# Attention's output projection by seven products with fewer accumulating transfers, another price for their queue in the plan, and the columns of sinks written by ScalarE or VectorE

## The chip, the cores and the metric

The kernel runs on one core of a Trainium2 chip. The metric is the device time of one execution in microseconds. Three executions of the kernel before took 2039.61, 2040.94 and 2041.01 us; the median is 2040.94 us. Line numbers are those of the kernel before.

## What is computed

A network of two layers on 1024 tokens of width 1024, in float32: layer 0 mixes by sliding-window attention with sinks, layer 1 by a gated recurrence (HGRN2), and each is followed by an MLP with a squared ReLU. The change lies in layer 0's attention:

```python
qkv = h @ w_qkv + b_qkv                       # 16 query heads of 64, 4 key/value heads
scores = einsum(q_blocks, k_band) * HEAD_DIM ** -0.5      # a block of 128 tokens sees itself and the block before
m = maximum(max(scores, axis=-1), sink)
e = exp(scores - m)
probs = e / (sum(e, axis=-1) + exp(sink - m))
out = einsum(probs, v_band)
x = x + out.reshape(bsz, seq, Q_DIM) @ w_o    # the output projection
x = x + square(relu(rmsnorm(x) @ w_up)) @ w_down
```

## The kernel before, in words

**Products.** TensorE (PE) multiplies float32 as three passes of a rounded high part and a low rest (`mm3`, L505): high by high, high by low, low by high. Every operand is therefore split into two tiles: ScalarE (ACT) casts the high part, VectorE (DVE) subtracts it (`weight_split` for weights into tiles `wh` and `wl`, `split` for activations). A tile is 128 by 512, or 256 KB.

**Seven products.** The output projection (`o_proj`, L1473) takes 2 by 2 blocks of tokens and channels by a scheme of seven products in place of eight (Strassen's, in Winograd's form). Products 1, 2 and 4 use blocks of the weight as they are; 5, 6, 3 and 7 use sums of blocks: 5 the sum of two, 6 the same with a third added, 3 the same with the fourth added, 7 another sum of two. The order is 1, 2, 5, 3, 6, 7, 4 (L1476), each over four slices `p` of the contracted channels, with four banks of PSUM each: products 1, 2, 5, 6 and 7 in the banks `p` (the list `main`), products 3 and 4 in the banks `q` (the list `side`). `proj_weight` (L1454) makes a weight: the sums are made by transfers. `dma_sum` (L455) loads the first block through SyncE's queue (SP) and adds the others with accumulating transfers, `dma_add` (L452), which GpSimd (POOL) issues: the transfer reads the destination and writes the sum back. For each `p`, product 5 has one such transfer, 6 one more into the same tile, 3 three, and 7 one: 24 in all. The tile of product 5 (`kept[p]`) goes on to product 6.

The operands of the token side are sums too: tiles `t[p]` and `b11[p]` get other heads' outputs added, 14 times by `dma_add` and twice by VectorE. A part of the residual `x` is added by 8 more accumulating transfers.

**Attention around it.** `attend` (L1381) goes through four groups of four heads, two groups at a time (a pair `gp`), in two halves of the tokens. The queries of a pair are written to DRAM by the projection (`queries`, `rows_out`, L1276) in ten stores, and read back in eight loads of 256 KB (the stacks) when the pair begins. `attend_block` (L1413) handles one block of one group: a tile `m` out of six buffers holds the scores, and its last column the sinks, which POOL writes (`self.ts("Pool", ...)`, L1419); then come the scores on PE, copies and masks on ACT and DVE, the exponentials, the transposes, and in `values` the products with the values. For the second half of the tokens, `attention` (L1563) interleaves the blocks with the last slices of the QKV products and with the first products of the output projection. After them the MLP's operands are made (`mlp_first`, and `finish`, which also uses accumulating transfers, tiles `t`).

**The order.** All of this is written into a list, and a planner (`Schedule`, L160) turns it into one order: a forward pass over modelled engines with a cost for each operation, then a backward pass that gives each a latest time, four times over. `SUM` is the time from the end of a `dma_add`'s issue to its landing, `LOAD` and `STORE` those of SP's transfers; the third argument of `self.op` before the tiles' own is the time on the issuing queue (900 for a `dma_add`). Engines take their instructions in the order planned, and one that waits holds all behind it on its engine. Tiles come from a fixed number of buffers (`a` 60, `t` 18, `m` 6, `wr` 6, four banks each of `p` and `q`), so the plan also sets who waits for a buffer.

Of the kernel before, what the change touches and what calls it, by code (L numbers as in the profile page):

```python
# [15 lines left out]
ALU = mybir.AluOpType  # L16
AX = mybir.AxisListType

P = 128
# [4 lines left out]
TH = T // NH  # L24
# [113 lines left out]
WEIGH = 1.0  # L138
DRAIN = {"whole": 200.0, "columns": 200.0}
LOAD, STORE = 4200.0,3200.0  # L140
SUM = 6400.0
HALF = {"ACT": 125.0, "DVE": 105.0}
READERS = {"ACT": "DVE", "DVE": "ACT"}
TABLES = {AF.Sqrt: "sqrt", AF.Sin: "sin", AF.Exp: "exp", AF.Tanh: "exp"}
# [239 lines left out]
class Net:  # L384
    def __init__(self, ctx, tc, io):
        self.nc, self.io = tc.nc, io
        self.s = Schedule()
        self.n = 0
        self.x = None
        self.pool = ctx.enter_context(tc.tile_pool(name="sb", bufs=1))  # L390
        self.pp = ctx.enter_context(tc.tile_pool(name="ps", bufs=1, space=bass.MemoryType.PSUM))
        self.dram = ctx.enter_context(tc.tile_pool(name="dr", bufs=1, space=bass.MemoryType.DRAM))
        nc = self.nc
        self.par = self.const((P, N_PAR))
        self.ones = self.const((P, P))
        self.memset(self.ones, 1.0)
        self.mean = self.const((P, 1))
        self.memset(self.mean, 1.0 / D)
        self.eps = self.const((P, 1))
        self.memset(self.eps, EPS)  # L400
        zero = self.t(F32, (P, P))
        self.memset(zero, 0.0)
        self.warm(zero)
        self.ident = self.const((P, P))
        self.square = [self.const((P, BPH)) for _ in range(NH)]
        self.op("Pool", nc.gpsimd.affine_select, [self.ident], [zero], 300,
                self.ident, zero, [[-1, P]], ALU.not_equal, 1.0, base=0, channel_multiplier=1)
# [15 lines left out]
    def a(self, dt=F32, shape=(P, TH)):  # L423
        return self.tile("a", BUFS["a"], shape, dt)
# [22 lines left out]

    def dma(self, out, in_, nbytes, least=450.0, late=0.0):
        tail = LOAD if isinstance(out, View) and out.buf.tag[0] != "d" else STORE
        self.op("SP", self.nc.sync.dma_start, [out], [in_], max(least, nbytes / 320.0), out, in_, tail=tail + late)  # L450

    def dma_add(self, out, y):  # L452
        self.op("Pool", self.nc.gpsimd.dma_start, [out], [out, y], 900.0, out, y, accum_op=ALU.add, tail=SUM)

    def dma_sum(self, out, x, *more):  # L455
        self.dma(out, x, 4 * P * TH)
        for y in more:
            self.dma_add(out, y)

# [953 lines left out]
    def attend_block(self, g, n, stacks):  # L1413
# [2 lines left out]
        tok = slice((n % BPH) * P, (n % BPH) * P + P)  # L1416
        ks, kl = self.ks[i][g].only(*((m, k) for m in (n - 1, n) for k in (0, HD))), self.kl[i][g].only(n - 1, n, "o")
        m = self.t(F32, (P, 4, P + 2), "m")
        self.ts("Pool", m[:, :, P : P + 1], self.sink[:, 4 * g : 4 * g + 4].unsqueeze(2), 1.0, None, ALU.mult, None, 4)  # L1419
        scores = [self.psum("q").rearrange("p (h s) -> p h s", h=2) for _ in range(2)]  # L1420
        for h in range(4):
            self.mm(scores[h // 2][:, h % 2], stacks[h][:, tok], ks[:, c], h % 2 == 0, False, 2 * P)
# [20 lines left out]
        if n:  # L1443
            y = self.t(F32, (P, 4, P))
# [9 lines left out]
    def proj_weight(self, name, p, kept):  # L1454

        a = lambda i, k: self.io["wo"][k, p, :, i]
        self.s.lead = LEAD
        if name in (1, 2, 4):
            z = self.raw(a(*{1: (0, 0), 2: (0, 1), 4: (1, 1)}[name]))
        elif name == 5:  # L1460
            z = kept[p] = self.a()
            self.dma_sum(z, a(1, 0), a(1, 1))
        elif name == 6:
            z = kept[p]
            self.dma_add(z, a(0, 0))
        else:
            z = self.a()
            self.dma_sum(z, a(0, 0), a(1, 0), *((a(1, 1), a(0, 1)) if name == 3 else ()))
        w = self.weight_split(z)
        self.s.lead = 0  # L1470
        return w

    def o_proj(self, out, b):  # L1473
# [3 lines left out]
        main = [self.psum() for _ in range(HK)]  # L1477
# [59 lines left out]
        yield from product(3, side, True)  # L1537
        yield from product(6, main, False)
        for m in range(HK):
            z = self.a()  # L1540
            self.copy(z, main[m])
            self.dma_add(z, self.io["x"][1, m])
            later.append(z)
        for m in range(HK):
            self.x[m][1] = later[m]
# [17 lines left out]
    def attention(self, layer):  # L1563
        self.v, self.dv, self.ks, self.kl = [], [], [None] * 3, [None] * 3
        out = [{}, {}]
        ahead = self.first_loads()
        h = [self.scaled(layer, 0)]
        self.attention_constants()
        run(self.qkv(0, *h[0], ahead))
        self.load_x([1])  # L1570
        h.append(self.scaled(layer, 1))
        rest = self.qkv(1, *h[1])
        for k, _ in enumerate(self.attend(0, out[0])):
            for _ in range((k + 1) * 18 // 16 - k * 18 // 16):
                next(rest)
        tiles = [[out[0][2 * k + p // 2, p % 2] for p in range(HK)] for k in range(2)]
        proj, first = self.o_proj(out, tiles), self.mlp_first(layer)
        side = chain(rest, proj)
        left = 6 + 13
        for k, _ in enumerate(self.attend(1, out[1])):  # L1580
            for _ in range((k + 1) * left // 16 - k * left // 16):
                next(side)
        for k in range(14):
            next(proj)
            if k % 3 == 2:
                next(first)
        run(proj)
        run(first)


    def hgrn_constants(self):
# [513 lines left out]
def run(pieces):  # L2105
    for _ in pieces:
        pass
# [92 lines left out]
```

## Time and profile before

| what | value |
|---|---|
| median of three runs | 2040.94 us |
| the profiled execution's own time | 2040.05 us |
| its span, first to last instruction | 2038.3 us |
| PE busy in the span | 2001.9 us, 98% |
| DVE, ACT and POOL busy | 1803.7, 1316.2 and 125.7 us |
| accumulating transfers (queue q0) | 24.65 MB, 6.9% of the 16 DMA engines' span |
| all of SP's transfers (queue q1) | 503.99 MB, 73.0% |
| mean granted clock of PE | 0.993 |

In the trace, names of tiles stand without their numbers (`a`, `t`, `m`, `q`), `in_wo` is the weight of the output projection, `in_up` that of the MLP, `d` a tile in DRAM, `out<-in` the direction. `POOLq` and `SPq` are issues of transfers. Nearly all instructions have line 438, since one helper issues them, so they are told apart by engine, tiles and time. The attention with its output projection lies between about 85 and 312 us of the span, the first MLP's products begin at about 314 us.

### The profile page before, as it was taken

Reading aid. Unit: us, or ns where it says so; the run is one execution under the profiler, and the core shown is the slowest. Engines: PE = TensorE matmul, PEld = TensorE weight load, DVE = VectorE, ACT = ScalarE, POOL = GpSimd, SP = SyncE. Lnnn points to the kernel's source line nnn. Section 1 sums busy time; section 2 is a strip of 40 time slices with the busy share of each in tenths; the row PEclk is TensorE's granted clock in tenths of the full one; section 3 lists DMA queues with packets and bytes.
Section 4 is the critical chain, followed back from the end, with each engine's and each line's share of the span. In section 5 each row is a group of like instructions: output and inputs, shape, how many; then the busy total and the mean of one; then the engine's idle time right before and its main releaser. Section 6 shows DMA issues by size and latency. Waiting matters only on the chain.

```text
span 2038.3 us, 40062 instructions
## 1 busy us (share of the span) xinstructions
PE 2001.9 (98%) x13772; PEld 1698.9 (83%) x13772; DVE 1803.7 (88%) x3639; ACT 1316.2 (65%) x2765; POOL 125.7 (6%) x223
## 2 busy tenths in 40 slices
PE   9999898999999999999999999999899999999998
PEld 8887676899998888888888888888789999888887
DVE  7878778999998978989999999999899999887985
ACT  7777766767766544656666666766776777444573
POOL 2001431000001000000000000001000001100000
PEclk9999899999999999999999999999999999999999
DMA  7848999888879977855888888989888889996812
GB/s 247 268 143 242 250 203 281 270 278 282 294 259 342 335 244 236 276 168 175 282 282 286 284 293 310 316 299 313 271 273 288 270 290 289 349 314 213 268 58 84
DMA packets 296348, 531.23 MB, mean 261 GB/s; under 512 B 34256, under 2 KB 42832, under 8 KB 296144
## 3 DMA queue, kind: packets, MB, share of 16 engines
q1 hardware_dynamic: 282464, 503.99, 73.0%
q0 software_dynamic: 13536, 24.65, 6.9%
q8 instruction: 109, 1.79, 0.4%
q14 instruction: 95, 0.78, 0.1%
q10 hardware_dynamic: 144, 0.02, 0.0%
HBM read 412.04 MB, written 110.72 MB: 256 GB/s over the span
## 4 chain that ended last, share of the span: by engine, by line
PE 89%; DMA 4%; DVE 4%; ACT 2%; issue 1%; SPq 0%; POOL 0%; DVEq 0%; ACTq 0%; POOLq 0%
PE p L438 48%; PE q L438 41%; DMA d<-t 2%; DVE t L438 2%; ACT t L438 1%; DMA a<-d 1%; DVE m L438 1%; DVE wl L438 1%; DMA a<-in_wo 1%; DMA a<-a 0%; ACT a L438 0%; DVE a L438 0%; ACT wh L438 0%; SPq L438 0%; DMA a<-in_x 0%
## 5 line engine op out<-in xcount | busy, mean ns | idle before, releaser
L438 PE MATMUL p<-a,wh 128*128 128x512 f32 (+1 forms) x3056 | 852.1, 363 | 4.8 <-ACT a L438 4.5
L438 PE MATMUL q<-a,wh 128*128 128x512 f32 x2084 | 650.1, 393 | 12.5 <-ACT t L438 10.4
L438 PEld LDWEIGHTS p<-a,wh 128*128 128x128 f32 x3056 | 544.3, 189 | 90.8 <-ACT a L438 5.2
L438 PE MATMUL p<-a,wl 128*128 128x512 f32 (+1 forms) x1528 | 549.1, 362 | 0.4 <-DVE wl L438 0.4
L438 PEld LDWEIGHTS q<-a,wh 128*128 128x128 f32 x2084 | 388.4, 189 | 92.5 <-ACT t L438 12.1
L438 PE MATMUL q<-a,wl 128*128 128x512 f32 x1040 | 405.1, 391 | 0.0
L438 PEld LDWEIGHTS p<-a,wl 128*128 128x128 f32 x1528 | 287.7, 189 | 43.6 <-DVE wl L438 0.8
L438 ACT CAST wh<-m 128x512 fp32r<-128x512 f32 (+1 forms) x354 | 212.5, 604 | 159.7 <-PE q L438 93.0
L438 ACT CAST wh<-wr 128x512 fp32r<-128x512 f32 (+1 forms) x304 | 180.8, 602 | 140.0 <-PE p L438 86.4
L438 DVE TENSOR_TENSOR wl<-m,wh 128x512 fp32r<-128x512 f32 (+1 forms) x354 | 235.2, 668 | 39.7 <-ACT wh L438 35.9
L438 PEld LDWEIGHTS q<-a,wl 128*128 128x128 f32 x1040 | 196.3, 189 | 41.0
L438 DVE TENSOR_TENSOR wl<-wr,wh 128x512 fp32r<-128x512 f32 (+1 forms) x304 | 200.3, 664 | 34.1 <-ACT wh L438 29.1
L438 DVE TENSOR_TENSOR t<-t,t 128x512 f32<-128x512 f32 (+3 forms) x382 | 215.8, 586 | 12.5 <-DMA t<-d 5.8
L438 ACT ACTIVATE t<-t 128x512 f32<-128x512 f32 x294 | 184.0, 631 | 48.8 <-DVE t L438 44.1
L438 DVE TENSOR_TENSOR a<-t,a 128x512 fp32r<-128x512 f32 (+1 forms) x261 | 173.6, 684 | 17.9 <-PE q L438 8.5
L438 ACT CAST a<-t 128x512 fp32r<-128x512 f32 x181 | 109.3, 617 | 43.5 <-DMA t<-d 26.4
L438 DVE TENSOR_TENSOR t<-t,p 128x256 f32<-128x256 f32 x288 | 116.9, 415 | 17.2 <-PE p L438 13.8
L438 ACT COPY t<-q 128x512 f32<-128x512 f32 (+2 forms) x254 | 111.7, 442 | 25.6 <-PE q L438 16.4
L438 ACT CAST a<-a 128x512 fp32r<-128x512 f32 x140 | 85.4, 620 | 42.2 <-DVE a L438 39.5
L438 DVE TENSOR_TENSOR a<-a,a 128x512 fp32r<-128x512 f32 (+2 forms) x157 | 105.0, 679 | 6.9 <-ACT a L438 3.8
L438 DVE TENSOR_TENSOR m<-wr,wr 128x512 f32<-128x512 f32 (+1 forms) x152 | 97.2, 642 | 1.8 <-DMA wr<-in_up 1.3
L438 PE MATMUL p<-t,wh 128*128 128x256 f32 x480 | 90.7, 283 | 0.0
(142 smaller groups left out, 2364.9 us busy)
## 6 DMA issues: line engine op xcount, KB each, us to landing
t<-d SPq DMA_DIRECT2D x584, 256.0 KB
a<-d SPq DMA_DIRECT2D x350, 256.0 KB
d<-t SPq DMA_DIRECT2D x318, 256.0 KB
wr<-in_up SPq DMA_DIRECT2D x172, 256.0 KB
wr<-in_down SPq DMA_DIRECT2D x160, 256.0 KB
wr<-in_win SPq DMA_DIRECT2D x68, 256.0 KB
d<-a SPq DMA_DIRECT2D x64, 256.0 KB
wr<-in_wqkv SPq DMA_DIRECT2D x48, 256.0 KB
```

The source lines that it names most:

```text
L438: fn(*[place(a) for a in args], **{k: place(v) for k, v in kw.items()})
```

## The change

- `proj_weight`: product 3's weight is no longer summed by transfers. Its fourth block is loaded raw, and VectorE adds it to `kept[p]` (the sum of three that product 6 uses) into a tile `m`. Product 6's accumulating transfer is listed right after product 5's weight has been split, not when product 6's weight is asked for. The 24 accumulating transfers become 12, SP's loads stay 24.
- `o_proj`: four of the eight residual tiles are loaded through SP and added by VectorE from PSUM, where before ScalarE copied the product and an accumulating transfer added `x`.
- `attend_block`: the 32 columns of sinks are copies by ScalarE or VectorE, as the planner chooses, not by POOL (as planned: 22 and 10).
- the plan: a `dma_add` costs 2050 on POOL (900 before) and lands 4000 after that (6400 before); the first load of a `dma_sum` is given 1500 more; every SP transfer listed between the first QKV pass and the end of `attention` 1500 more (`slow`). These numbers change no work, only the order, in the whole program.

```diff
-SUM = 6400.0
+SUM, SLOW = 4000.0, 1500.0
...
-        self.op("SP", self.nc.sync.dma_start, [out], [in_], max(least, nbytes / 320.0), out, in_, tail=tail + late)
+        self.op("SP", self.nc.sync.dma_start, [out], [in_], max(least, nbytes / 320.0), out, in_, tail=tail + late + self.slow)
...
-        self.op("Pool", self.nc.gpsimd.dma_start, [out], [out, y], 900.0, out, y, accum_op=ALU.add, tail=SUM)
+        self.op("Pool", self.nc.gpsimd.dma_start, [out], [out, y], 2050.0, out, y, accum_op=ALU.add, tail=SUM)
...
-        self.dma(out, x, 4 * P * TH)
+        self.dma(out, x, 4 * P * TH, late=1500.0)
...
-        self.ts("Pool", m[:, :, P : P + 1], self.sink[:, 4 * g : 4 * g + 4].unsqueeze(2), 1.0, None, ALU.mult, None, 4)
+        self.copy(m[:, :, P : P + 1], self.sink[:, 4 * g : 4 * g + 4].unsqueeze(2), 4, ("ACT", "DVE"), False)
...
         elif name == 5:
             z = kept[p] = self.a()
             self.dma_sum(z, a(1, 0), a(1, 1))
+            w = self.weight_split(z)
+            self.dma_add(z, a(0, 0))
+            self.s.lead = 0
+            return w
         elif name == 6:
             z = kept[p]
-            self.dma_add(z, a(0, 0))
+        elif name == 3:
+            z, y = self.t(tag="m"), self.raw(a(0, 1))
+            self.tt("any", z, y, kept[p], ALU.add)
         else:
             z = self.a()
-            self.dma_sum(z, a(0, 0), a(1, 0), *((a(1, 1), a(0, 1)) if name == 3 else ()))
+            self.dma_sum(z, a(0, 0), a(1, 0))
...
         for m in range(HK):
-            z = self.a()
-            self.copy(z, main[m])
-            self.dma_add(z, self.io["x"][1, m])
+            z = residual(m, 1)
+            self.tt("DVE", z, main[m], z, ALU.add)
             later.append(z)
```

The new order differs in most rows of the program, mostly by a few places. Three places matter below. In the rows, the number behind `_` tells tiles apart.

SP's queue around the loads of the stacks of the second pair, second half of the tokens (tiles `a663` and on, from the queries' DRAM tile `d7778`; `in_wo` and `in_up` are weights). Before:

```order
L438 DMA d7778_2750<-t612_2832 16x8x512
L438 DMA a825_2883<-in_wo 128x512
L438 DMA a828_2891<-in_wo 128x512
L438 DMA wr885_2905<-in_wo 128x512
L438 DMA wr888_2918<-in_wo 128x512
L438 DMA wr907_2929<-in_up 128x512
L438 DMA wr910_2940<-in_up 128x512
L438 DMA a663_2956<-d7778_2750 128x512
```

and now:

```order
L438 DMA d7778_2583<-t609_2735 16x8x512
L438 DMA a770_2759<-in_wo 128x512
L438 DMA d7778_2583<-t612_2756 16x8x512
L438 DMA wr782_2788<-in_wo 128x512
L438 DMA wr824_2803<-in_wo 128x512
L438 DMA wr828_2866<-in_wo 128x512
L438 DMA a663_2888<-d7778_2583 128x512
```

Six loads stood between the last store of queries and the first stack, now three; the load `a770` of product 5's last weight has moved from ahead of all ten stores to between the last two.

POOL's queue from the sums for product 3 to the operand of product 6's first slice (`a264`, to which `a671` is added; `a822` and `a828` are tiles of product 3, `a770` the tile of products 5 and 6, last slice, the others tiles of product 7). Before:

```order
L438 DMA a822_3060<-in_wo 128x512
L438 DMA a854_3199<-in_wo 128x512
L438 DMA a828_2891<-in_wo 128x512
L438 DMA a861_3263<-in_wo 128x512
L438 DMA a822_3060<-in_wo 128x512
L438 DMA a864_3311<-in_wo 128x512
L438 DMA a770_2666<-in_wo 128x512
L438 DMA a264_1546<-a671_3387 128x512
```

and now:

```order
L438 DMA a759_2706<-in_wo 128x512
L438 DMA a851_3015<-in_wo 128x512
L438 DMA a858_3058<-in_wo 128x512
L438 DMA a865_3203<-in_wo 128x512
L438 DMA a770_2759<-in_wo 128x512
L438 DMA a264_1576<-a671_3373 128x512
```

The three adds into `a822` and `a828`, each of which waits for the one before it into the same tile, are gone from ahead of `a264`, and so is the fourth tile of product 7 (`a864`), whose successor now stands nine rows behind.

PE's matmuls where product 3 (banks `q`) and product 6 (banks `p`) meet; `wh835` before and `wh839` now are product 6's first weight, `a786` and `a787` the operand split from `a264`. Before:

```order
L438 MATMUL q819_3554<-a788_3424,wh782_3354 128x512
L438 MATMUL q819_3554<-a789_3435,wh782_3354 128x512
L438 MATMUL q819_3554<-a788_3424,wl783_3403 128x512
L438 MATMUL p613_2644<-a786_3549,wh835_3359 128x512
L438 MATMUL p614_2652<-a786_3549,wh835_3359 128x512
```

and now:

```order
L438 MATMUL q820_3539<-a789_3413,wl784_3407 128x512
L438 MATMUL q819_3530<-a793_3424,wh825_3440 128x512
L438 MATMUL q819_3530<-a794_3449,wh825_3440 128x512
L438 MATMUL q819_3530<-a793_3424,wl826_3476 128x512
L438 MATMUL q820_3539<-a793_3424,wh825_3440 128x512
L438 MATMUL q820_3539<-a794_3449,wh825_3440 128x512
L438 MATMUL q820_3539<-a793_3424,wl826_3476 128x512
L438 MATMUL p613_2566<-a787_3519,wh839_3317 128x512
```

Six matmuls of product 3's second slice now stand ahead of product 6's first.

More of the change, by code (lines that the diff above doesn't have):

```diff
@@ L388, in __init__ @@
         self.n = 0
-        self.x = None
+        self.x, self.slow = None, 0.0
         self.pool = ctx.enter_context(tc.tile_pool(name="sb", bufs=1))
@@ L1569, in attention @@
         run(self.qkv(0, *h[0], ahead))
+        self.slow = SLOW
         self.load_x([1])
@@ L1588, in attention @@
         run(first)
+        self.slow = 0.0
     def hgrn_constants(self):
```

## Prediction

> **What bounds the kernel now.** The page first: TensorE (PE) is busy nearly all the time, so only its idle time and its clock can be won.
>
> ```profile
> span 2038.3 us, 40062 instructions
> PE 2001.9 (98%) x13772; PEld 1698.9 (83%) x13772; DVE 1803.7 (88%) x3639; ACT 1316.2 (65%) x2765; POOL 125.7 (6%) x223
> ```
>
> Idle are 2038.3 - 2001.9 = 36.4 us. Next the waits of PE (total, times, longest) and its timeline, which says where they lie:
>
> ```profile
> PE q L438 <- DMA a<-d: 8.7, 2, 7.5
> PE p L438 <- ACT a L438: 4.5, 1, 4.5
> ```
>
> ```profile
> 218.76 0.79 PE L438 MATMUL q<-a,a 128*128 128x256 f32 x2 [7.46 <-DMA a<-d]
> 220.79 1.65 PE L438 MATMUL q<-a,a 128*128 128x256 f32 x6 [1.24 <-DMA a<-d]
> 263.31 2.50 PE L438 MATMUL p<-a,wh 128*128 128x512 f32 x5 [4.54 <-ACT a L438]
> 313.78 0.70 PE L438 MATMUL q<-a,wh 128*128 128x512 f32 x2 [1.58 <-ACT a L438]
> 342.57 1.22 PE L438 MATMUL q<-a,wh 128*128 128x512 f32 x2 [5.01 <-ACT t L438]
> ```
>
> Call them A (the two at 218.76 and 220.79: the first scores of the second pair wait for the stacks), B (263.31: product 6's first operand) and C (313.78 and 342.57: the MLP's start). Together 19.8 of the 36.4 us lie between 195 and 345 us, just where the change works. After a long wait PE also runs at a lower granted clock (the column behind POOL's in the windows):
>
> ```profile
> 219.00:225.00 6.00, 4.76 (x18) 3.60 (x18) 1.48 (x3) 1.68 (x4) 0.86 (x1) 0.50 1.09 316
> 264.00:268.00 4.00, 4.00 (x17) 3.19 (x16) 2.48 (x4) 3.39 (x7) 2.63 (x3) 0.72 0.89 177
> 343.00:347.00 4.00, 4.00 (x10) 3.04 (x10) 3.79 (x6) 0.57 (x2) 0.00 (x0) 0.50 0.83 267
> 400.00:700.00 300.00, 299.94 (x1794) 268.14 (x1793) 279.27 (x575) 196.87 (x367) 13.83 (x16) 1.00 0.90 298
> ```
>
> At half clock 4.76 us of matmuls would have been 2.4; the loss is 2.4 behind A, 4.00 x 0.28 = 1.1 behind B, 2.0 behind C. So A costs 7.46 + 1.24 + 2.4 = 11.1 us, B 4.54 + 1.1 = 5.6, C 1.58 + 5.01 + 2.0 = 8.6. From 400 to 700 us, where the MLP's plan is shuffled too, PE never waits: nothing to win there.
>
> **Part by part: A.** The chain of waits and SP's timeline show what A waits for:
>
> ```profile
> 208.61 12.14 DMA a<-d
> ...
> 241.31 10.64 DMA a<-in_wo
> ...
> 253.58 9.03 DMA a<-a
> ```
>
> ```profile
> 189.51 12.72 SPq L438 DMA_DIRECT2D d<-t  x10
> 202.32 2.15 SPq L438 DMA_DIRECT2D a<-in_wo  x2
> 204.53 0.90 SPq L438 DMA_DIRECT2D wr<-in_wo  x2
> 205.53 1.86 SPq L438 DMA_DIRECT2D wr<-in_up  x2
> 207.48 9.65 SPq L438 DMA_DIRECT2D a<-d  x8
> ```
>
> The queries' ten stores end at 202.2, six loads go ahead of the stacks, and a stack then takes 12.14 us to land. Why so long: the DMA engines are full, though few bytes move. Compare two stretches (last columns: clock, DMA share, GB/s), and the price of each queue:
>
> ```profile
> 195.00:220.00 25.00, 16.80 (x102) 12.69 (x100) 15.79 (x30) 15.55 (x50) 8.68 (x11) 0.90 1.01 251
> 300.00:340.00 40.00, 35.76 (x155) 28.49 (x153) 34.45 (x57) 28.05 (x52) 7.03 (x8) 1.00 1.05 316
> ```
>
> ```profile
> q1 hardware_dynamic: 282464, 503.99, 73.0%
> q0 software_dynamic: 13536, 24.65, 6.9%
> ```
>
> A plain 256 KB transfer takes 0.730 x 2038.3 / 503.99 x 0.262 = 0.77 us of all 16 engines, an accumulating one 0.069 x 2038.3 / 24.65 x 0.262 = 1.50. The change removes 12 + 4 accumulating ones and adds four plain ones: 24 - 3 = 21 us less transfer work between 180 and 300.
>
> In the new order three things move A. First, the 32 scores of the first pair that stood ahead of the last QKV matmuls now stand behind them:
>
> ```profile
> 177.89 2.81 PE L438 MATMUL q<-a,a 128*128 128x256 f32 x22
> 180.53 0.40 PE L438 MATMUL p<-a,wh 128*128 128x512 f32 x1
> ```
>
> 22 take 180.53 - 177.89 = 2.64 us, so 32 take 3.8: the queries, and with them the stores, can come 3.8 us earlier. Second, three loads fewer stand ahead of the stacks (2.3 us) and, of product 3's twelve accumulating transfers, three or four stood in POOL's order beside them (three: 4.5 us), 6.8 together; transfers overlap, so I count half, 3.4. Third, against it, eight matmuls fewer stand ahead of the first scores; by the chain's row
>
> ```profile
> 795.65 43.52 PE p L438 x192
> ```
>
> one takes 0.227, so the stacks are wanted 1.8 us sooner. Net 3.8 + 3.4 - 1.8 = 5.4 of the 8.7 us; 3.3 would be left, none with the whole 6.8. I take 2.0 left, between the two; a wait that short costs no clock, as the 1.58 at 313.78 cost none. **A: -9.1** (bounds -11.1 and 0).
>
> **B.** POOL's timeline and PE's, around product 6's first operand:
>
> ```profile
> 252.51 1.75 POOL L438 DMA_DIRECT2D a<-in_wo  x2 [3.06 <-DVE t L438]
> 253.58 2.46 POOL L438 DMA_DIRECT2D a<-a  x2
> ```
>
> ```profile
> 243.46 3.67 PE L438 MATMUL q<-t,a 128*64 128x256 f32 x32
> ```
>
> Of ACT's copies behind those matmuls,
>
> ```profile
> L438 ACT ACTIVATE a<-q 128x256 f32<-128x256 f32 x32 | 10.4, 381 | 7.7 <-PE q L438 7.7
> ```
>
> four make the heads to be added: they leave PE at 247.1 and need some 1.5 us on ACT, yet the add is issued at 253.58: POOL was held by product 3's chained adds (the 10.64 us of `a<-in_wo` above, landing at 251.95). With them gone, what is left ahead is the add into product 5's last tile, which waits for that tile's split: the issue comes 2 to 4 us earlier, I take 2.5. It still takes 9.03 us to land. Six matmuls of product 3 now stand ahead on PE, 1.4 us of cover. 4.54 - 2.5 - 1.4 = 0.6; since A's gain brings PE's part sooner than the transfers', I take 2.0 left: **B: -3.6** (bounds -5.6 and +2).
>
> The Trainium skill's page "DMA: Bandwidth & Descriptors", section "Anatomy of one DMA — SWDGE (gpsimd) path", gives a transfer from GpSimd's queue 2.0 us plus its bytes over 436 GB/s, by which 256 KB would be an estimated 2.6 us. By it the operand would be there 6.4 us sooner than the 9.03 of the chain, nothing of B would be left, and the sum would be 2.0 us lower. The trace disagrees, in the chain and in the issues (last number: median us to landing), so the rows decide:
>
> ```profile
> a<-in_wo POOLq DMA_DIRECT2D x24, 256.0 KB, 7.7
> a<-a POOLq DMA_DIRECT2D x14, 256.0 KB, 6.3
> ```
>
> **New work.** Four adds on DVE for product 3 and four from PSUM, four copies less on ACT, and 32 columns of sinks on ACT and DVE:
>
> ```profile
> L438 DVE TENSOR_TENSOR a<-a,a 128x512 fp32r<-128x512 f32 x20 | 13.3, 685 | 0.9 <-ACT a L438 0.8
> L438 ACT COPY a<-p 128x512 f32<-128x512 f32 x8 | 4.7, 593 | 0.5 <-PE p L438 0.3
> L438 POOL TENSOR_SCALAR m<-c 128x4 f32<-128x4 f32 x32 | 16.2, 509 | 109.1 <-PE q L438 101.9 <-DVE m L438 5.8 <-DMA c<-in_sinks 0.6
> L438 DVE RECIPROCAL sm<-sm 128x4 f32<-128x4 f32 x33 | 5.8, 174 | 7.1 <-ACT m L438 7.1
> ```
>
> DVE gets 8 x 0.685 = 5.5 us, ACT loses 4 x 0.593 = 2.4. A column has no row on these engines; the nearest, 128x4 on DVE, takes 0.174 us, so 32 take 5.6 us in place of POOL's 16.2. Most lie where PE has other work, but just ahead of A both engines are full:
>
> ```profile
> 180.00:200.00 20.00, 19.70 (x108) 16.11 (x109) 19.04 (x38) 19.21 (x65) 7.17 (x11) 1.00 0.90 223
> ```
>
> There five columns and their delay fall on the queries' chain: 0 to 3 us, I take **+0.5**. Product 3's adds are put at nothing: its first two slices stand ahead of product 6, while B still waits for a transfer; without that cover each would cost its 0.685.
>
> Product 7's last weight is now loaded after the adds to `t` and added nine rows behind `a264`; its PE row is 36 matmuls later than before, 8.2 us. That is room for an add at 7.7 us behind a load that lands in time, not for the chain's 12.14 and 10.64: 0 to 4, **+1.0**.
>
> **C** hangs on the end of product 4, which stays at its row, on the store and reload of four tiles behind it and the adds to `t`: **0** (bounds -4 and +4, about half its price either way). The rest of the program is reordered by the new prices with PE at 100% in most windows: 0, bounds -1 and +2.
>
> **Sum.** -9.1 - 3.6 + 0.5 + 1.0 = -11.2 against the profiled execution's 2040.05: 2028.9. The median of the runs is 0.9 above that execution, so 2029.7 in its terms.
>
> **Rivals.**
>
> *The next one is late (17%).* With A gone PE arrives 9 us sooner at operands whose transfers do not: product 5's added operand, B, product 7's weight. Against it: A's wait held those chains too. For it: a landing of 9.03 and a stretch with the DMA engines at 1.01. A quarter to two thirds of A and B (12.7 us) is given back: 2033 to 2038, two fifths of it within 0.2%.
>
> *The transfers are the bound (8%).* DMA shares of 1.01 and 1.05 would mean that the stretch can't shrink. For it: the shares. Against it: 316 GB/s at 1.05 beside 251 at 1.01, that is, accumulating takes room without moving bytes. Waits then only move: 2037 to 2041.
>
> *Everything goes (10%).* A, B and most of C vanish: 2040.9 - 11.1 - 5.6 - 4 = 2020.
>
> *Slower: ACT held by a late add (10%).* Product 5's last load now stands behind nine of ten stores; its accumulating transfer heads POOL's queue, behind it the adds to `t`; and in ACT's order the cast of the first such sum now stands ahead of the second pair's score copies (behind the first of them before). If the load takes the stacks' 12.14 us and the add the longest landing seen here,
>
> ```profile
> DMA to landing us min/median/max: 3.3/7.3/13.1
> ```
>
> 25 us pass from an issue near 197 (the stores' 202.2 less 3.8, and one store): 222. The scores are wanted from 209 on (211 less 1.8), and PE has some 2 us of other matmuls: it stands 11 us with 2.4 of clock, 13.4, against A's 11.1; POOL's queue being late, B stays, and the five columns and the adds on a held ACT and DVE cost 2.5: 2040.9 + 2.3 + 2.5 = 2046. From about 20 us for load and add together it eats all that A gives; at twice 7.3 it costs some 2 us, which is in what I left of A.
>
> **How the numbers follow.** Forecast 55% (2024 to 2034, time 2029.7), everything goes 10%, the next one late 17%, transfers bound 8%, ACT held 10%. A measurement of this kernel can tell about 0.2%, 4.1 us: faster is below 2036.9, slower above 2045.0. Faster 0.55 + 0.10 + 0.10 + 0.02 = 0.77; same 0.07 + 0.06 + 0.01 = 0.14; slower 0.09. The range leaves out the upper half of "ACT held", the top of the two middle rivals and the lower half of "everything goes": 2020 to 2040.
>
> **What would show it.** A right: PE's wait for `a<-d` below 3 us, the ten stores ending 3 us or more earlier against the last QKV matmul, the stack's 12.14 shorter. B right: POOL's idle time for `a<-in_wo` gone, the add issued within 4 us of the head's last matmul. Wrong, if PE's idle time between 195 and 345 us stays above 15 us, whoever it waits for; if ACT shows a wait of 4 us or more for an added tile near 210; if C grows; or if waits appear from 400 to 700 us.

## The result, and the profile after

The changed kernel takes 2020.87 us (median of five, 2017.38 to 2021.09) against 2041.01 of the kernel before, measured beside it: a ratio of 0.9896, 95% interval 0.9880 to 0.9912. That is 20 us, 1.0%, faster; forecast were 11.2. A few executions fell into a slow state (one of the kernel before took 9556.04 us here); the ratios, here and below, leave them out. The profiled execution took 2021.09, 18.96 less than that of before, and its page says in what form:

```profile
span 2019.3 us, 40022 instructions
PE 1996.8 (99%) x13772; PEld 1694.8 (84%) x13772; DVE 1806.0 (89%) x3657; ACT 1316.4 (65%) x2783; POOL 99.1 (5%) x175
q0 software_dynamic: 11232, 20.45, 5.8%
```

PE idles 2019.3 - 1996.8 = 22.5 us (36.4 before), and its same 13772 matmuls take 5.1 us less: idle time and clock, 13.9 + 5.1 = 19.0. PE's timeline after, all waits of 1 us or more behind the first 10 us:

```profile
210.69 0.39 PE L438 MATMUL q<-a,a 128*128 128x256 f32 x1 [1.12 <-ACT t L438]
299.14 0.50 PE L438 MATMUL p<-a,wh 128*128 128x512 f32 x1 [1.77 <-DVE a L438]
315.18 0.73 PE L438 MATMUL q<-a,wh 128*128 128x512 f32 x2 [1.99 <-ACT t L438]
338.99 0.73 PE L438 MATMUL q<-a,wh 128*128 128x512 f32 x2 [1.24 <-ACT t L438]
1412.38 0.73 PE L438 MATMUL q<-a,wh 128*128 128x512 f32 x2 [1.69 <-ACT t L438]
1418.34 0.74 PE L438 MATMUL q<-a,wh 128*128 128x512 f32 x2 [2.94 <-ACT t L438]
```

No wait for `a<-d` is left, and between 211 and 297 us PE waits for nothing: A is down to 1.12 (for another operand), B is gone. Of C 1.77 + 1.99 + 1.24 = 5.0 us are left. The waits at 1412 and 1418 us are not new; the kernel before waits 0.91 at 1429.85 and

```profile
1437.35 1.22 PE L438 MATMUL q<-a,wh 128*128 128x512 f32 x2 [4.48 <-ACT t L438]
```

The windows (PE's busy time first, the granted clock after POOL's column) show where the clock still drops:

```profile
212.00:220.00 8.00, 8.00 (x62) 6.06 (x62) 6.42 (x14) 6.00 (x25) 4.54 (x7) 1.00 1.09 303
316.00:321.00 5.00, 5.00 (x16) 3.97 (x15) 4.62 (x8) 4.97 (x11) 0.00 (x0) 0.66 1.10 263
```

Not behind A any more, but behind the wait at 315: 5.00 x 0.34 = 1.7 us. Since both programs issue as many matmuls of each kind, they can also be followed by count along the order: the last of product 5 starts at 256.54 before and at 245.23 now, 11.3 us earlier; the first of product 6 at 263.31 and 248.18, 15.1 earlier; the last of product 4 at 311.81 and 294.03, 17.8 earlier; one in the MLP at 448.93 and 428.93, 20.0 earlier. After it 1.0 is given back on balance (one new wait, 0.51 at 608.93, lies between 400 and 700 us, where PE waited for nothing before). So all of the gain lies before 450 us.

How A went is in SP's timeline (the stores of the queries, the loads behind them, the stacks):

```profile
178.58 0.55 SPq L438 DMA_DIRECT2D d<-t  x1
...
191.32 1.64 SPq L438 DMA_DIRECT2D d<-t  x1
193.01 5.21 SPq L438 DMA_DIRECT2D wr<-in_wo  x3
198.46 4.52 SPq L438 DMA_DIRECT2D a<-d  x8
```

The last store is issued at 191.3, before at 201.6; the eight stacks in 4.52 us, before in 9.65; and by the trace's landing records the first stack lands at 203.4, before at 218.7: 15.3 us earlier, where the forecast had 3.8 + 3.4 = 7.2. PE wants it at 208.15, so 4.7 us of slack stand where PE waited 7.46.

### The profile page after: what moved, and what is told of

Its sections match the earlier page's. It is cut to its first block, busy times and chain, and to the rows that moved or that the text cites. A ratio compares the mean times of both kernels' runs of the same rounds, so it can differ in the third digit from the quotient of the medians.

```text
span 2019.3 us, 40022 instructions
## 1 busy us (share of the span) xinstructions
PE 1996.8 (99%) x13772; PEld 1694.8 (84%) x13772; DVE 1806.0 (89%) x3657; ACT 1316.4 (65%) x2783; POOL 99.1 (5%) x175
## 4 chain that ended last, share of the span: by engine, by line
PE 89%; DMA 4%; DVE 3%; ACT 2%; issue 1%; SPq 0%; DVEq 0%; ACTq 0%; POOLq 0%
PE p L438 49%; PE q L438 40%; DMA d<-t 2%; DVE t L438 2%; ACT t L438 1%; DVE wl L438 1%; DVE m L438 1%; DMA m<-in_down 1%; DVE a L438 0%; ACT wh L438 0%; DMA a<-a 0%; ACT a L438 0%; DMA a<-in_x 0%; DMA t<-d 0%; ACT m L438 0%
## 5 line engine op out<-in xcount | busy, mean ns | idle before, releaser
L438 ACT ACTIVATE t<-t 128x512 f32<-128x512 f32 (+1 forms) x294 | 183.9, 633 | 60.6 <-DVE t L438 54.7
```

Source lines behind the costliest of these rows:

```text
L438: fn(*[place(a) for a in args], **{k: place(v) for k, v in kw.items()})
```

## The experiments

All theories agree that A and B went; they differ in what took them away, and in what a transfer costs. One is that accumulating transfers hold up the stores and the stacks, in full; the other, that they overlap with them, and that the early stores (the score matmuls moved by `slow`) make A. The expectations number their theories each for itself: in *Early stores alone*, *All but the early stores* and *Product 3 by transfers again*, theory 1 is that the stores make A and theory 2 that the removed transfers do; in *The weights alone*, the spare transfers and what follows, theory 1 is that the transfers count. Each kernel was timed beside the kernel before on the same chip; times are medians.

### One part alone, and all but one

*Early stores alone* (the kernel before, with):

```diff
-SUM = 6400.0
+SUM, SLOW = 6400.0, 1500.0
-... tail=tail + late)
+... tail=tail + late + self.slow)      # slow = SLOW during the attention
```

> The kernel before with one number of the plan changed: every SP transfer listed during the attention is planned 1500 later (slow). No work changes; 30 score matmuls of the first pair move from ahead of the last QKV matmuls to behind them, as in the changed kernel. Theory 1 (the early stores pay for A): the ten stores of queries end about 7 to 9 us earlier than at 202.3, PE's wait for a<-d near 219 falls from 8.7 to below 2 us and its clock loss (2.6) goes; B (4.5 us of wait at 263) and C stay within 2 us of what they were. Time 2029 to 2032, against 2040.9. Theory 2 (the removed accumulating transfers pay for A, the order of the scores does little): the wait for a<-d stays at 5 us or more, time 2036 to 2041.

2033.1 us, ratio 0.9965 (0.9952 to 0.9978). A is gone, but not as theory 1 said: the last store is issued at 199.65, only 1.9 us sooner, and the stacks even later than before (208.0). Two other things take A away. The plan sets the first scores of the second pair behind 1310 matmuls, where 1276 stood ahead of them before, so PE wants the first stack at 214.7, 3.4 us later; and the stack lands at 213.3, 5.4 us sooner. Without the later place some 2.0 of wait would have been left. POOL's timeline, at and after that place, shows why it lands sooner, and PE's what it costs:

```profile
201.64 0.97 POOL L438 DMA_DIRECT2D a<-in_wo  x1
207.48 0.22 POOL L438 TENSOR_SCALAR m<-c 128x4 f32<-128x4 f32 x1 [4.87 <-PE p L438]
210.57 0.90 POOL L438 DMA_DIRECT2D a<-in_wo  x1 [2.86 <-PE p L438]
...
247.52 1.77 POOL L438 DMA_DIRECT2D a<-in_wo  x2 [6.48 <-DMA a<-in_wo]
248.59 2.48 POOL L438 DMA_DIRECT2D a<-a  x2
```

```profile
256.59 2.50 PE L438 MATMUL p<-a,wh 128*128 128x512 f32 x5 [6.43 <-ACT a L438]
```

A column of sinks and then an add itself wait for PE and hold POOL's queue: from 202.6 to 210.6 no accumulating transfer is started, and between 210.0 and 217.8 none lands, just while the stacks do. The adds come behind it, and B grows from 4.54 to 6.43, with more clock. What A gave is partly given back, and the time stands between the two ranges.

*All but the early stores* (the changed kernel, with `SLOW` at 0):

```diff
-SUM, SLOW = 4000.0, 1500.0
+SUM, SLOW = 4000.0, 0.0
```

> The changed kernel with slow at 0: the 12 and 4 accumulating transfers are gone, the sinks are on ScalarE and VectorE, but the scores stand ahead of the last QKV matmuls again. Theory 1: the stores end within 2 us of 202.3 again, the first scores of the second pair wait 5 us or more (they are wanted 1.6 us sooner, and three loads fewer stand ahead of the stacks), with 2 to 2.6 us of clock: 7 to 10 us above the changed kernel's 2020.9, 2028 to 2031. B is gone all the same. Theory 2: the wait for a<-d stays below 3 us, time 2021 to 2025.

2026.04 us, ratio 0.9930 (0.9917 to 0.9943), again between the two ranges. Its profiled execution took 2021.97, so the trace, PE's timeline here, doesn't show most of what the median has more than the changed kernel:

```profile
210.44 0.51 PE L438 MATMUL q<-a,a 128*128 128x256 f32 x2 [1.81 <-DMA a<-d]
212.42 0.74 PE L438 MATMUL q<-a,a 128*128 128x256 f32 x4 [1.01 <-DMA a<-d]
214.50 0.62 PE L438 MATMUL q<-a,a 128*128 128x256 f32 x3 [0.90 <-DMA a<-d]
304.57 0.50 PE L438 MATMUL p<-a,wh 128*128 128x512 f32 x1 [4.38 <-DVE a L438]
```

With the scores where they were, A still falls to 3.7 us, without a loss of clock, and B is gone. The last store is issued at 197.8, 3.8 us sooner than before, though PE's last QKV matmul ahead of it stands on the same row.

*The weights alone* (the kernel before, with the new `proj_weight`):

```diff
         elif name == 5:
             ...
+            w = self.weight_split(z)
+            self.dma_add(z, a(0, 0))
+            ...
+            return w
         elif name == 6:
             z = kept[p]
-            self.dma_add(z, a(0, 0))
+        elif name == 3:
+            z, y = self.t(tag="m"), self.raw(a(0, 1))
+            self.tt("any", z, y, kept[p], ALU.add)
```

> The kernel before with the new proj_weight alone: 12 accumulating transfers fewer, four raw loads and four adds on VectorE; plan's numbers, sinks and residual as before. The QKV matmuls, the scores and the first scores of the second pair stand on the same places as before. Theory 1 (what held the stacks are accumulating transfers that share the DMA engines with the stores and the stacks, and they count in full, 1.5 us each): the first stack, which lands at 218.7 before, lands 6 to 8 us sooner, the wait for a<-d falls from 8.7 to 3 us or less and its clock loss of 2.6 to 1 or none; B goes, since POOL's chained adds go: 2026 to 2030. Theory 2 (they count by half, as forecast, and the early stores are needed for the rest): the first stack lands 3 to 4 us sooner, 4 to 6 us of wait with 1.5 to 2.5 of clock stay, B goes: 2031 to 2035.

2030.0 us, ratio 0.9949 (0.9936 to 0.9962). The first scores have the place in PE's order that they had, and the twelve transfers alone bring the first stack from 218.7 to 209.6, 9.1 us sooner. PE's timeline and SP's:

```profile
213.86 0.62 PE L438 MATMUL q<-a,a 128*128 128x256 f32 x3 [0.94 <-DMA a<-d]
...
304.75 0.79 PE L438 MATMUL p<-a,wh 128*128 128x512 f32 x1 [3.82 <-DVE a L438]
333.05 1.19 PE L438 MATMUL q<-a,wh 128*128 128x512 f32 x4 [2.98 <-ACT t L438]
```

```profile
203.93 7.33 SPq L438 DMA_DIRECT2D a<-d  x8
```

A is 0.94, B none: theory 2 falls, half a count would have left 4 us or more (theory 1 had the stack 6 to 8 us sooner, so it came sooner still). Its profiled execution is 6.7 us longer than the changed kernel's. Of that 3.3 stand at product 6's first matmul (251.51 against 248.18), a wait of 1.53 for DVE at 242 among them; the rest lies behind 295: a wait of 3.82 with 7.00 x 0.42 = 2.9 us of clock in the window 305 to 312, C's 2.98, and 6.39 at 1422, against the changed kernel's 5.0 + 1.7 there and 1.69 + 2.94 from 1412 on.

The stacks of these kernels side by side (issues from SP's timeline, landings from the trace's landing records, in us):

| kernel | last store issued | first stack issued | landed | PE wants it | PE waits for stacks |
|---|---|---|---|---|---|
| before | 201.6 | 207.5 | 218.7 | 211.3 | 8.7 |
| early stores alone | 199.7 | 208.0 | 213.3 | 214.7 | 0 |
| all but early stores | 197.8 | 201.9 | 210.4 | 208.6 | 3.7 |
| the weights alone | 198.5 | 203.9 | 209.6 | 210.8 | 0.9 |
| all (changed kernel) | 191.3 | 198.5 | 203.4 | 208.1 | 0 |

The bytes of the accumulating queue from 180 us to about the first stack's landing, before (180 to 219) and with the new weights alone (180 to 210), follow it (packets, MB, share of the 16 engines):

```profile
q0 software_dynamic: 1605, 2.94, 43.7%
```

```profile
q0 software_dynamic: 711, 1.30, 25.3%
```

*Product 3 by transfers again* (all else as changed):

```diff
         elif name == 3:
-            z, y = self.t(tag="m"), self.raw(a(0, 1))
-            self.tt("any", z, y, kept[p], ALU.add)
+            z = self.a()
+            self.dma_sum(z, a(0, 0), a(1, 0), a(1, 1), a(0, 1))
```

> The changed kernel with product 3's weight summed by three accumulating transfers again (12 in all come back, and four loads less one each stay), everything else as changed. Theory 1 (stores pay for A, the chained adds on POOL's queue make B): the wait for a<-d stays below 3 us; an add for product 6's first operand is held behind the chained adds, PE waits 3 to 5 us for an ACT-cast operand near 250 and loses 1 to 1.5 us of clock: 2024.5 to 2027.5. Theory 2 (transfers pay for A): 12 x 1.5 us of all DMA engines come back, the wait for a<-d returns at 4 us or more beside B: 2030 to 2036.

2025.83 us, ratio 0.9929 (0.9915 to 0.9944): in theory 1's range. There is no wait for `a<-d`; the first stack lands at 204.5, 1.0 later than in the changed kernel. Of B only 0.76 is back; a wait of 2.12 is for product 3's own weight, whose chained adds are back, and C has grown. PE's timeline:

```profile
247.99 0.50 PE L438 MATMUL p<-a,wh 128*128 128x512 f32 x1 [0.76 <-ACT a L438]
...
251.56 1.19 PE L438 MATMUL q<-a,wh 128*128 128x512 f32 x4 [2.12 <-ACT wh L438]
...
332.98 0.50 PE L438 MATMUL q<-a,wh 128*128 128x512 f32 x1 [3.47 <-DVE a L438]
```

*The residual by transfers again:*

```diff
-            z = residual(m, 1)
-            self.tt("DVE", z, main[m], z, ALU.add)
+            z = self.a()
+            self.copy(z, main[m])
+            self.dma_add(z, self.io["x"][1, m])
```

> The changed kernel with four residual tiles added by accumulating transfers again (and copied by ScalarE). If C shrank because these four transfers no longer stand in the way of the stores that free the MLP's t tiles: 2 to 3 us of waits come back between 295 and 345, time 2022.5 to 2024.5. If C shrank only because the stores and adds ahead of it were issued earlier by the rest of the change: no more than 1 us, 2020 to 2022.

2020.84 us, ratio 0.9904 (0.9889 to 0.9919): in time, nothing to be told from the changed kernel: four accumulating transfers more behind product 6 cost nothing. The trace says less plainly so. Its profiled execution (2022.68) waits 6.3 us between 295 and 345, against 5.0, and loses 3.4 of clock there, against 1.7.

*The sinks on POOL again:*

```diff
-        self.copy(m[:, :, P : P + 1], self.sink[...].unsqueeze(2), 4, ("ACT", "DVE"), False)
+        self.ts("Pool", m[:, :, P : P + 1], self.sink[...].unsqueeze(2), 1.0, None, ALU.mult, None, 4)
```

> The changed kernel with the columns of sinks written by POOL again. If sinks on POOL hold its queue (a column waits for a free m tile, and the adds behind it wait with it): adds into product 5's and 6's operands are issued later than in the changed kernel, PE waits 2 to 5 us more for an ACT-cast operand between 230 and 260, time 2023 to 2028. If the columns only cost their own time: 2020 to 2022.

2024.57 us, ratio 0.9918 (0.9905 to 0.9931). The time is in the first case's range, the reason isn't: between 10 and 296 us PE has no wait of 0.25 us or more (the plan sets the first scores of the second pair 45 matmuls later here). The loss lies at the MLP's start, in PE's timeline:

```profile
300.49 0.50 PE L438 MATMUL p<-a,wh 128*128 128x512 f32 x1 [3.86 <-DVE a L438]
322.30 1.22 PE L438 MATMUL q<-a,wh 128*128 128x512 f32 x2 [3.79 <-ACT t L438]
```

### What a transfer costs beside the stacks

The order of the changed kernel is kept; four transfers of 256 KB of the weight into spare DRAM tiles are put on POOL's queue when the first stack is issued. Nobody reads them. The edit, shortened:

```diff
         for op in ops:
+            if op is self.mark:          # the first stack of the last pair
+                for k in range(4):
+                    nc.gpsimd.dma_start(spare[k], wo[0, k, :, 0], accum_op=ALU.add)
             op.ways[op.engine][0]()
```

> The changed kernel in the same order, with four accumulating transfers of 256 KB more on POOL's queue, from the weight into spare DRAM tiles that nobody reads, put there just when the first stack is issued. Theory 1 (accumulating transfers take the DMA engines from the stacks in full): the first two stacks, which land at 203.4 and 204.3, land 3 to 6 us later, the eighth (212.1) 5 to 7 us later; the add into product 5's operand lands later as well, so PE waits 3 to 7 us near 210: 2023 to 2028. Theory 2 (they only take POOL's time to issue, 0.87 us each, or run beside the stacks): stacks within 2 us of the changed kernel, 2020 to 2023.

The same without `accum_op`:

> The same, but the four transfers are plain copies into the spare tiles: the same bytes read, the same queue and the same four issues, nothing accumulated. Theory 1: about half the DMA time of the accumulating ones, stacks 1 to 3 us later than in the changed kernel, time 2020.5 to 2023 and below that of the accumulating ones by 2 us or more. Theory 2: the same as the accumulating ones within 1 us.

And with `accum_op`, but behind the next two adds on POOL's queue:

```diff
             self.dma_add(t[p], n01[p])
+            if p == 1:
+                self.s.mark = self.s.ops[-1]   # and the four are issued behind it
```

> The changed kernel with the same four spare accumulating transfers as in the run with four accumulating ones ahead, but two places later on POOL's queue: behind the two adds into product 5's first operands, not ahead of them. The bytes and the issues are the same. If the 8.05 us of wait there came from the DMA engines being full (whoever stands where): the adds issued near 200.4 land 3 us or more later than at 209.0, PE waits 4 to 8 us near 211, time 2024 to 2028. If it came from the place in POOL's queue (the operand's adds issued behind four others and served behind them): the adds land within 2 us of 209.0, PE waits 3 us or less, the later stacks still land 3 to 6 us later but are wanted only at 225, time 2020.5 to 2023.5.

Accumulating: 2028.25 us, ratio 0.9940 (0.9927 to 0.9953). Plain: 2023.32, 0.9916 (0.9902 to 0.9930, which overlaps with the changed kernel's), 0.3 above theory 1's range and 4.9 below the accumulating ones. Accumulating, behind: 2021.19, 0.9898 (0.9882 to 0.9915). Against the changed kernel that is +7.4, +2.4 and +0.3 us. The chains of waits around 210, for the accumulating four, the plain four and the four behind (`a<-a` is the add into product 5's operand, from issue to landing):

```profile
200.89 14.77 DMA a<-a
```

```profile
200.08 10.73 DMA a<-a
```

```profile
200.04 8.84 DMA a<-a
```

And PE's timelines, in the same order (the helper has line 440 in these kernels):

```profile
217.36 0.58 PE L440 MATMUL q<-a,a 128*128 128x256 f32 x1 [8.05 <-ACT t L440]
```

```profile
212.51 0.39 PE L440 MATMUL q<-a,a 128*128 128x256 f32 x1 [3.27 <-ACT t L440]
```

```profile
210.58 0.39 PE L440 MATMUL q<-a,a 128*128 128x256 f32 x1 [1.38 <-ACT t L440]
```

In the changed kernel the add is issued at 200.40 and takes 8.59, and PE waits 1.12. The eight stacks, which land at 203.4 to 212.1 there, land at 203.6, 205.7, 207.8, 209.7, 211.8, 213.8, 215.8 and 217.9 beside the accumulating four, and up to 214.6 beside the plain four: the eighth is 5.8 and 2.5 us late, as the prices say (4 x 1.50 = 6.0, 4 x 0.77 = 3.1). So theory 1 holds for the eighth stack: by then they count in full, and an accumulating one counts about twice a plain one of the same size on the same queue (these wrote to DRAM; in the kernel they write to SBUF). It doesn't hold for the first two, which it put 3 to 6 us later: they are 0.2 and 1.4 later beside the accumulating four, and the delay grows from stack to stack. Nor did the stacks' delay cost PE anything, since they had the slack; what cost was the place in POOL's queue. Four transfers ahead of an add that is waited for cost 7.4 us, the same four behind it 0.3, though they are issued only 2.7 us later (from 201.38, not 198.65) and the last stacks are nearly as late (the eighth lands at 216.3).

### The prices in the plan, and two tries for more

*The old prices of the sums* (`slow` kept):

```diff
-SUM, SLOW = 4000.0, 1500.0      # and 2050 on POOL, late=1500.0
+SUM, SLOW = 6400.0, 1500.0      # and 900 on POOL, late=0.0
```

> The changed kernel with the old prices of the sums (SUM 6400, 900 on POOL, no 1500 for the first load); slow stays. The QKV matmuls, the stores and the stacks keep their places, so A and B stay gone by either theory. Theory 1 (the removed transfers pay; the prices of the sums do little): 2020 to 2022.5, PE's waits from 200 to 290 below 3 us in all. Theory 2 (the new prices put the adds in time): adds issued in the wrong order hold POOL, 2 us or more of waits for an ACT-cast operand come back between 205 and 260: 2023 to 2027.

2024.98 us, ratio 0.9925 (0.9912 to 0.9938). PE waits 0.73 at 210 and for nothing more until 296, so A and B don't need the new prices. Behind that stands a wait of 4.10 for DVE at 300.96. But its profiled execution took 2019.96, less than the changed kernel's, and its others up to 2025.69, so where the median's difference lies isn't shown.

*Product 7's weight by loads and an add, too:*

```diff
-            self.dma_sum(z, a(0, 0), a(1, 0))
+            y = self.raw(a(1, 0))
+            self.dma(z, a(0, 0), 4 * P * TH, late=1500.0)
+            self.tt("any", z, z, y, ALU.add)
```

> The changed kernel with product 7's weight made like product 3's: two plain loads and an add on VectorE or ScalarE's partner in place of one load and one accumulating transfer, four times. By theory 1 four accumulating transfers (6.0 us of the DMA engines) become four plain ones (3.1), but in the changed kernel the stacks land 4.7 us before they are wanted, so nothing is left to win at A and B; the wait of 1.1 near 210 may go: 2019 to 2021. If VectorE, 90% busy there, is the bound by now, four adds of 0.685 cost 1 to 3 us around 260 to 300: 2021 to 2024.

2024.12 us, ratio 0.9935 (0.9920 to 0.9950): slower than the changed kernel, and 0.1 above the second range, though the four adds aren't seen as waits for DVE from 260 to 300. The wait near 210 is gone, one of 0.88 at 258 has come, and those for DVE and ACT at the MLP's start are 3.12 and 2.96.

*`slow` at 3000:*

```diff
-SUM, SLOW = 4000.0, 1500.0
+SUM, SLOW = 4000.0, 3000.0
```

> The changed kernel with slow at 3000 in place of 1500: the QKV matmuls keep their place, the first scores of the second pair stand 11 matmuls earlier (wanted 2.9 us sooner), the stacks stand four places later in SP's queue. If A's slack of 4.7 us is real: no wait of more than 2 us for a<-d, time 2018 to 2023, set by what happens to C. If the slack is taken up: 2 to 4 us of wait for a<-d near 206, 2022 to 2026.

2023.65 us, ratio 0.9924 (0.9911 to 0.9936). The slack is real, and used up: PE comes to the first scores at 204.8, 3.3 us sooner, the first stack lands at 205.4, 2.0 later, and PE waits 0.76, put down to DVE. So the first case holds, but its range missed by 0.65. The MLP's start takes back what came sooner:

```profile
301.02 0.80 PE L438 MATMUL p<-a,wh 128*128 128x512 f32 x1 [5.02 <-DVE a L438]
326.37 0.73 PE L438 MATMUL q<-a,wh 128*128 128x512 f32 x2 [3.75 <-ACT t L438]
```

No kernel tried is faster than the changed one (that with the old residual takes the same time).

## Why the prediction was too small, point by point

**The step that failed.** The sum kept back 2.0 us of A and 2.0 of B, added 1.5 for new work and product 7, and took nothing for C and the rest. None of what was kept back or added was there, but for 1.1 us at A, for another operand. Under A's 2.0 two terms were too small: the early stores (3.8 forecast, 10.3 measured) and the transfers counted by half (3.4 forecast, 5.0 measured).

**What bounds, and A's place: right.** The gain lies where the prediction looked, between 180 and 345 us, as idle time and as clock. The prices of the clock were read too low: the windows behind A, B and C end before the stretches of half clock do, or begin behind their start. By the clock records, with half of PE's busy time in the whole stretches, the loss is 2.65, 1.5 and 2.8 us there, not 2.4, 1.1 and 2.0, so 1.4 more could be won. The prices below are the prediction's.

**A: forecast -9.1, measured 11.1 to 1.1, that is -10.0.** The three movements were named rightly, but two of them were sized too small. Against 7.2 us the first stack came 15.3 sooner: the last store was issued 10.3 sooner (forecast 3.8), the loads ahead of the stacks gave nothing (5.9 us from the last store to the first stack before, 7.1 now), and the landing shrank from 11.2 to 5.0, so that "transfers overlap, so I count half" gave 3.4 where 5.0 came. What brings the last store 10.3 us sooner isn't settled: `slow` alone brings 1.9, all but `slow` 3.8, and the two together make 5.7. With the twelve transfers alone gone the first stack came 9.1 sooner. It is also wanted 3.1 us sooner, not 1.8. Since only 8.7 of it could be used, the error costs 1.0 us of the sum: that A's number came near is owed to this bound, not to its terms. That A goes by the removed transfers alone (0.9 left) and by `slow` alone (none left, by its later place for the scores too) was not foreseen: either was enough.

**B: forecast -3.6, measured -5.6, all of it.** The step that failed is "since A's gain brings PE's part sooner than the transfers', I take 2.0 left". PE came 10.6 us sooner (258.77 to 248.18), the operand's add landed 18.4 sooner (262.6 to 244.2). POOL's wait for `a<-in_wo` (a name that loads and sums of the weight share) between 176 and 300 us fell from 30.4 us to 2.4; POOL's waits before and after:

```profile
POOL a L438 <- DMA a<-in_wo: 30.4, 5, 15.1
```

```profile
POOL a L438 <- DMA a<-in_wo: 2.4, 1, 2.4
```

The timelines of PE and POOL after show the heads' matmuls and the add for product 6's first operand:

```profile
232.78 3.67 PE L438 MATMUL q<-t,a 128*64 128x256 f32 x32
...
248.18 0.39 PE L438 MATMUL p<-a,wh 128*128 128x512 f32 x1
```

```profile
237.42 2.12 POOL L438 DMA_DIRECT2D a<-a  x2
```

The matmuls end at 236.45 and the add is issued 1.0 us later (before 253.58 - 247.1 = 6.5): 5.5 sooner where 2.5 were taken. It lands at 244.2, and PE comes at 248.18, 4.0 us later. So B was POOL's queue, as the prediction said, but what held it last was misread. The 10.64 us of `a<-in_wo` that land at 251.95 are no chained add of product 3. POOL issues nothing at 241.31; SP does, and POOL's last chained add is the second of two that go out from 247.68 on. The timelines of SP and of POOL before:

```profile
241.31 1.43 SPq L438 DMA_DIRECT2D a<-in_wo  x1
```

```profile
247.68 1.76 POOL L438 DMA_DIRECT2D a<-in_wo  x2 [2.75 <-PE q L438]
```

It is a load, and the add that waits for it, issued at 252.51, is by POOL's order that of product 7's fourth tile. The chained adds held the queue to 248.3, that tile from there to 252.5. Both are gone from ahead of product 6's add in the new order. No run parts the two: the weights alone take all of B, with product 3's sums back the changed kernel waits 0.76 there, and early stores alone make B larger.

**New work: +0.5, none seen.** The stores that the five columns could have delayed end 10.3 us earlier, and no wait of PE follows from them; the last QKV matmul ends 4.4 us earlier (product 1's first starts at 177.97 in place of 182.37), 3.8 of them by the scores that moved. **Product 7: +1.0, none.** PE does not wait at any matmul of product 7 (272.5 to 283.2).

**C: forecast 0, measured 8.6 to 6.7, -1.9**, within its bounds. Whether the residual has a part in it isn't settled: with the old one the time is the same (2020.84), but the trace has more waits there. Waits and clock from 295 to 345 us come to 5 to 7 us in the four kernels with the changed kernel's order (itself and the three with spare transfers), and to 8 to 12 in every kernel with another order, by waits for DVE or for ACT. Which edit moves which of its chains isn't settled: they run through stores of `t` tiles, ACT and DVE, with the DMA engines at 1.04 or more from 295 to 320 us in each of the nine kernels in which that window was read.

**Rest: 0, measured -1.3 up to product 5's end** (11.3 less the 10.0 of A; 0.3 of it the wait at 198.65 of before, 0.25 the clock behind A that its window left out, the rest in no single wait)**,** with 1.0 given back after 450 us.

The sum: 1.0 (A) + 2.0 (B) + 0.5 + 1.0 + 1.9 (C) + 1.3 (the front) = 7.7, near the 7.8 us by which 19.0 exceeds 11.2; 1.2 more by 450 us (the clock behind B and C that the windows left out) and the 1.0 given back nearly cancel. The places and the waits hold; the sizes failed, six remainders each left on the cautious side as if they were independent. The traces speak against that: POOL's queue, ahead of PE at A, is ahead at B too. The time is that of the rival "everything goes", put at 2020, whose lower half was left out of the range, but not by its account alone: A and B went, of C 6.7 of 8.6 stayed, and what PE gained elsewhere made up for it.

**The other rivals.** "The next one is late" asked for a quarter to two thirds of 12.7 us back in waits; there is one, the 1.12 for product 5's added operand. "Transfers are the bound": the DMA share stays over 1 (1.09 from 212 to 220) and PE still works, so a full DMA share alone says nothing. "ACT held by a late add" is the same wait, real, but 1.12 us: ACT's cast waits 1.37 us for `a<-a` at 209.01, and the spare transfers show the way to the price it was given (8.05 of wait with four of them ahead).

**The page on transfers from GpSimd's queue.** By the Trainium skill ("DMA: Bandwidth & Descriptors", "Anatomy of one DMA — SWDGE (gpsimd) path") the add behind B would take an estimated 2.6 us. It now takes 6.8 (237.42 to 244.2), and B still went: the landing shrank by 2.3 us, and the issue came 5.5 sooner behind the heads' matmuls.

## What to carry to other kernels

Price an accumulating transfer in full where a queue beside it is full (the eighth load beside four of them came 5.8 us late, the first 0.2), and ask first who is queued behind it: four of them ahead of an add that is waited for cost 7.4 us, behind it 0.3. Where one cause (here a full queue of accumulating transfers) stands behind several waits, forecast them together, as they went together here. When a row of a chain carries a name that two queues share, find the issue at its start before saying whose it is. A full DMA share isn't a bound by itself; look at which transfer lands next and who wants it.

## What the runs showed of the hardware

**Two full queues take turns.** With POOL's queue full of accumulating transfers, those of SP's and of POOL's queue land one each about every 2.0 us: beside the accumulating four the stacks at 203.6, 205.7, 207.8, 209.7, and POOL's transfers at 205.5, 207.6, 209.7, 211.6. Before the change the first three stacks land at 218.7, 220.7 and 222.7, between POOL's at 218.4, 220.4 and 222.4; the fourth to sixth, as POOL's queue runs out (its next land at 224.5 and 227.4), at 223.9, 224.7 and 225.3. The shares of the engines from 195 to 215 us beside the accumulating four (packets, MB, share) show that the smaller number of bytes takes the larger part:

```profile
q0 software_dynamic: 1061, 1.95, 53.9%
q1 hardware_dynamic: 1842, 3.35, 50.0%
```

The Trainium skill, "DMA: Bandwidth & Descriptors", section "Queues, rings and completion order", has each engine go round the queues that have work, a packet at a time; the landings agree, though they don't show the packets.

**SP holds eight transfers at most in these programs.** SP's transfers use eight completion counters in turn, and an issue waits for the transfer eight places before it: before the change the sixth, seventh and eighth stack are issued at 212.76, 214.74 and 216.81, just behind landings at 212.7, 214.7 and 216.7. So slow landings of weights delay the issue of stacks that depend on none of them. The last store of the queries is no case of it: its counter was free from 198.0 on, and it was issued at 201.6.

**The clock falls in steps.** In the trace's clock records half clock lasts 10.2 us around A, 3.4 around B, 6.8 at 342 and 3.4 at 1437 before the change, and 3.4 at each of the waits at 315 and 1418 after it: the wait of 1.99 us at 315 cost 1.7 more, that of 1.24 at 339 none. The Trainium skill's page "TensorE: Matmul & The Clock Gate", section "What's actually happening", gives a window of 3413 ns that runs free of the kernel; the lengths agree.
